# Projecting attention values and state-space gates with tokens on the partitions

## The chip, the cores and the metric

One NeuronCore of a Trainium2 chip runs the whole program. TensorE (PE) multiplies, VectorE (DVE) and ScalarE (ACT) work on its results in PSUM and on SBUF, GpSimd (POOL) helps, and SyncE (SP) issues most transfers. The metric is the device time of one execution in microseconds, the median of several.

## The reference

Two layers of a decoder trunk in float32, 512 tokens of 1024 features, batch 1. A layer, with W_in one projection whose columns are q, k, v, z, x, B, C, dt and two gates:

```python
x = x + 0.5 * swiglu(rms_norm(x, ffn1_norm[l]), ffn1_w_up[l], ffn1_w_down[l])
h = rms_norm(x, mix_norm[l])
q, k, v, z, xbc, dt_raw, gate_sb, gate_ssm = jnp.split(h @ w_in[l], IN_SPLITS, axis=-1)
y_sb = stick_breaking_attention(q, k, v) @ w_branch_sb[l]          # 4 heads of 128
y_ssm = mamba2_mixer(z, xbc, dt_raw, ...) @ w_branch_ssm[l]        # 24 heads of 64, 8 groups
x = x + (sigmoid(gate_sb) * y_sb + sigmoid(gate_ssm) * y_ssm) @ w_out[l]
x = x + 0.5 * swiglu(rms_norm(x, ffn2_norm[l]), ffn2_w_up[l], ffn2_w_down[l])
```

The mixer convolves x, B and C over four tokens per channel and applies silu, scans each group of three heads in chunks of 128 tokens, multiplies the result by silu(z), and normalises each group's 192 channels.

## The kernel before

**Layout.** Activations lie with features on the partitions: h is 8 tiles of 128 features by 512 tokens. A projection block (`project`) is 8 steps over the features; each step has three matmuls of 512 columns (`mm3`): every operand is split in a high part (hhi, whi) and a rest (hlo, wlo), and three of the four products are summed. The weights are the stationary operand (128x128), h the moving one, and the result, 128 features by 512 tokens, fills one PSUM tile "mm". The pool of these tiles has four, taken in turn: a block's tile is that of the block four earlier, and its first matmul waits until everything that reads the old one is done.

**Weights.** They come in units of up to 512 KB on SP's queue in the order of `unit_order`; ScalarE casts a unit to whi and VectorE subtracts (wlo, lines 259 and 261). Units are converted some blocks ahead.

**Order.** One thread of Python writes TensorE's stream block after block. What follows a block (scaling, convolution, attention, the scan) is a generator, given to `spawn`. After each step of a block `tick` advances all of them; so the order on every engine is set by how many ticks each generator lets pass (`yield n`). Engines run their own instructions in that order.

**The mixer.** q, k and v of four heads are projected in `qkv_order`. The first four blocks (q0, k0, q1, k1) are projected before the norm of x is known and scaled afterwards from PSUM by VectorE (lines 521 and 523, `scaled`). A v block is copied to SBUF by ScalarE and turned by `transposed` (line 834: four transposes on TensorE, which must go through PSUM), since attention needs tokens on the partitions; two splits (lines 380, 385) follow. Then come the 8 groups, 5 blocks each in GROUP_ORDER (3, 4, 0, 1, 2): B, C, x (128 columns), x and z (64 each), z (128), with two gate blocks between in the first six groups. `conv_block` does the convolution from PSUM: ScalarE the first tap (line 969), VectorE the others (line 972), then tanh on ScalarE (979) and the product that makes it silu on VectorE (989). Blocks 0 to 2 are transposed into "xz", x and z of the group by tokens; B also, in three quarters. `ssd_group` runs the scan of a group on all engines, in the end the norm (lines 1109 and 466 to 470, small operations, then 1119 on the normalised output), which is transposed back.

**The opening.** The first two blocks are computed while x and their weights arrive in pieces (`opening_loads`, `opening`, line 431).

Of the kernel before, what the change touches and what calls it, by code (L numbers as in the profile page):

```python
# [1 line left out]

# [56 lines left out]
NCONV = GROUPS * 4 * (KCONV + 1)  # L59


def group_cols(g):

    x0, z0 = OFF_X + g * GW, OFF_Z + g * GW
    b0, c0 = OFF_B + g * P, OFF_C + g * P
    return (list(range(x0, x0 + GW)) + list(range(z0, z0 + GW))
            + list(range(b0, b0 + P)) + list(range(c0, c0 + P)))
# [26 lines left out]
def unit_order(layer):  # L94
# [16 lines left out]
    for g in range(GROUPS):  # L111
        for i, c in enumerate(GROUP_ORDER):
            yield (layer, "grp", g, c), KB
            if g < EARLY and i in GATE_AT:
                yield (layer, GATE_AT[i], g), KB
    for m in range(EARLY, KB):
        yield (layer, "gs", m), KB
        yield (layer, "gm", m), KB
# [22 lines left out]
class Builder:  # L141
# [251 lines left out]
    def opening_loads(self):  # L393


# [3 lines left out]
        def weights(queue, i, cs):  # L399
            off, _ = self.units[self.keys[i]]  # L400
            src = self.wflat[off:off + KB * P * P].rearrange("(p f) -> p f", p=P)
            queue.dma_start(self.raw[i][:, cs], src[:, cs])
# [366 lines left out]
    def dt_stage(self, layer, ps):  # L769
# [54 lines left out]
        self.tok = self.t(mp, [P, NT, P], "tok", bufs=1)  # L824
# [12 lines left out]
    def qkv_parts(self, t, ps, normed, parts):  # L837
        scale = P ** -0.5 if t == "q" else None
        if normed and t != "v":
# [5 lines left out]
        if normed:  # L845
            self.nc.scalar.copy(r, ps)
        else:
            yield from self.scaled(r, ps, scale)
        yield 4 if t == "v" else 2
        if t == "v":  # L850
            r = self.transposed(r)
            yield 2
            two = self.pair(self.yt, ("yt", "yt"), (P, NT, P))
        else:
            two = self.pair(self.yt, ("yt", "yt"))
        yield from self.split(two, r)
        self.give("raw")
        parts[t] = two

# [5 lines left out]
    def attention(self, h, parts):  # L865
# [7 lines left out]
        at = [sum(SEQ - i * P for i in range(j)) for j in range(NT + 1)]  # L873
        spt = [self.t(mp, [P, at[NT]], "xz", F32R) for _ in range(2)]
        pzs, sps, ws, bufs, ready = {}, {}, {}, {}, set()

        def scores(j):
# [18 lines left out]
            yield from self.split([s[:, at[j]:at[j] + n] for s in spt], e)  # L896
            yield 2 if n < 300 else 3
            sps[j] = [s[:, at[j]:at[j] + n] for s in spt]
# [39 lines left out]
        while len(ws) < NT or "v" not in parts:  # L938
            yield 1
        yield 2  # L940
        v = parts["v"]
        po = self.t(self.ptr, [P, SEQ], "pt")
        for j in range(NT):
            self.mm3(po[:, j * P:], (v[0][:, j, :], v[1][:, j, :]), ws[j], j == 0, j == NT - 1,
# [6 lines left out]
    def conv_block(self, g, c, ps, proj):  # L951
# [5 lines left out]
        early = len(self.y_sb) < SBH or not self.dt_done  # L957
        src, scale = u, 1.0
        if c == 2:
            if early:  # L960
                nc.vector.tensor_copy(u, ps)
            else:
                src = ps
            scale = 0.5
            yield 1
        else:
            k0 = (g * 4 + (0, 1, None, 2, 3)[c]) * (KCONV + 1)
            tap = [self.conv[:, k0 + i:k0 + i + 1] for i in range(KCONV + 1)]
            nc.scalar.activation(u, ps, AF.Identity, scale=tap[KCONV - 1], bias=tap[KCONV])  # L969
            yield 2  # L970
            for i in range(1, KCONV):
# [456 lines left out]
```

## Time and profile before

| | |
|---|---|
| median of 3 runs | 2615.7 us (2614.91 to 2615.94) |
| the profiled execution | 2614.76 us |
| its span, first to last instruction | 2612.8 us |
| TensorE busy | 2593.7 us, 99% of the span |
| VectorE, ScalarE, GpSimd busy | 1752.5, 1298.2, 508.8 us |
| mean granted TensorE clock | 0.998 |

The busy time of an engine is the union of its instructions' times; a stretch in which TensorE is not busy is a wait. The profiled execution took 2.0 us more than its span. The mixer of layer 0 stands at about 356 to 860 us, that of layer 1 at about 1655 to 2155 us.

### The profile page before, as it was taken

To read this page: it belongs to the slowest core of one execution; us is meant where nothing else is said; L and a number is where in the kernel's file an instruction comes from. 1 tells how busy PE (TensorE), PEld (TensorE's weight loads), DVE (VectorE), ACT (ScalarE), POOL (GpSimd) and SP (SyncE) were. 2 spreads that over 40 slices of the span, in tenths; PEclk is the share of its full clock that TensorE was granted. 3 is DMA by queue.
4 is the path that set the end of the run, shared out by engine and by line. 5 is a ranking of instruction groups with operands and counts; after the bars stand their busy time and mean duration, and the time that the engine had idled before them with its cause. 6 is when DMAs were issued, how large, how long until landed. Compare 5 with 4: busy or idle time off the path is not lost.

```text
span 2612.8 us, 38174 instructions
## 1 busy us (share of the span) xinstructions
PE 2593.7 (99%) x15058; PEld 2294.1 (88%) x15058; DVE 1752.5 (67%) x2370; ACT 1298.2 (50%) x2095; POOL 508.8 (19%) x629
## 2 busy tenths in 40 slices
PE   9999999999999999999999999999999999999998
PEld 7898988888888889899998989888888888899997
DVE  7576876565665478585885858766666754775766
ACT  6343556655554255353553535566555643553434
POOL 1120201133232003021120312012332410021210
PEclk9999999999999999999999999999999999999999
DMA  5464442333323546463554644423333234464642
GB/s 186 138 155 138 122 137 77 102 109 105 113 89 100 163 145 162 137 182 110 160 141 126 176 126 130 134 77 107 97 117 105 97 101 157 137 179 131 175 122 81
DMA packets 104004, 336.37 MB, mean 129 GB/s; under 512 B 12128, under 2 KB 15456, under 8 KB 103824
## 3 DMA queue, kind: packets, MB, share of 16 engines
q1 hardware_dynamic: 91728, 293.22, 34.9%
q0 software_dynamic: 10944, 39.85, 8.6%
q8 instruction: 118, 1.93, 0.3%
q10 hardware_dynamic: 1152, 0.86, 0.1%
q14 instruction: 62, 0.51, 0.1%
HBM read 321.20 MB, written 12.68 MB: 128 GB/s over the span
## 4 chain that ended last, share of the span: by engine, by line
PE 93%; DVE 4%; ACT 1%; DMA 1%; issue 1%; POOL 0%; SPq 0%; DVEq 0%; ACTq 0%
PE mm L292 26%; PE mm L294 26%; PE mm L293 26%; PE pa L293 3%; PE pa L294 3%; PE pa L292 3%; PE pa L1071 1%; PE pt L834 1%; PE pa L908 1%; DVE wlo L261 1%; PE pa L1073 1%; PE pt L1056 1%; PE pt L1054 1%; DVE cv L972 0%; DMA x<-in_xT_dram 0%
## 5 line engine op out<-in xcount | busy, mean ns | idle before, releaser
L259 ACT CAST whi<-wraw 128x1024 fp32r<-128x1024 f32 (+2 forms) x434 | 434.2, 1001 | 592.9 <-PE mm L294 505.3
L292 PE MATMUL mm<-hhi,whi 128*128 128x512 f32 (+1 forms) x1856 | 679.6, 366 | 1.1 <-ACT hhi L480 1.1
L294 PE MATMUL mm<-hlo,whi 128*128 128x512 f32 (+1 forms) x1856 | 660.3, 356 | 0.1
L293 PE MATMUL mm<-hhi,wlo 128*128 128x512 f32 (+1 forms) x1856 | 658.6, 355 | 0.5 <-DVE wlo L261 0.5
L261 DVE TENSOR_TENSOR wlo<-wraw,whi 128x1024 fp32r<-128x1024 f32 (+2 forms) x434 | 542.3, 1250 | 168.2 <-ACT whi L259 167.5
L294 PEld LDWEIGHTS mm<-hlo,whi 128*128 128x128 f32 x1856 | 350.9, 189 | 52.0 <-DVE hlo L482 0.5
L293 PEld LDWEIGHTS mm<-hhi,wlo 128*128 128x128 f32 x1856 | 351.7, 189 | 44.4 <-issue 1.0
L292 PEld LDWEIGHTS mm<-hhi,whi 128*128 128x128 f32 x1856 | 351.5, 189 | 44.0 <-ACT hhi L480 1.5
L597 POOL TENSOR_TENSOR g<-g,rs 128x512 f32<-128x512 f32 x76 | 133.2, 1752 | 735.8 <-DVE g L604 715.1
L261 DVE TENSOR_TENSOR wlo<-s,whi 128x1024 fp32r<-128x1024 f32 x152 | 235.5, 1564 | 58.4 <-ACT whi L259 58.4
L292 PE MATMUL mm<-act,whi 128*128 128x512 f32 (+1 forms) x710 | 274.0, 386 | 0.0
L293 PE MATMUL mm<-act,wlo 128*128 128x512 f32 (+1 forms) x710 | 273.8, 386 | 0.0
L294 PE MATMUL mm<-act,whi 128*128 128x512 f32 (+1 forms) x710 | 273.6, 385 | 0.0
L292 PE MATMUL mm<-th,whi 128*128 128x256 f32 x912 | 258.1, 283 | 0.0
L293 PE MATMUL mm<-th,wlo 128*128 128x256 f32 x912 | 258.1, 283 | 0.0
L294 PE MATMUL mm<-tl,whi 128*128 128x256 f32 x912 | 258.1, 283 | 0.0
L259 ACT CAST whi<-s 128x1024 fp32r<-128x1024 f32 x152 | 159.0, 1046 | 100.4 <-PE mm L294 58.9
L623 DVE SCALAR_TENSOR_TENSOR x<-mm,x 128x512 f32<-128x512 f32 x93 | 64.0, 689 | 196.2 <-PE mm L294 196.2
L292 PEld LDWEIGHTS mm<-th,whi 128*128 128x128 f32 x912 | 175.1, 192 | 0.0
L293 PEld LDWEIGHTS mm<-th,wlo 128*128 128x128 f32 x912 | 175.1, 192 | 0.0
L294 PEld LDWEIGHTS mm<-tl,whi 128*128 128x128 f32 x912 | 175.1, 192 | 0.0
L972 DVE SCALAR_TENSOR_TENSOR cv<-mm,conv,cv 128x511 f32<-128x511 f32 (+2 forms) x192 | 142.3, 742 | 24.7 <-ACT cv L969 22.9
(275 smaller groups left out, 4566.6 us busy)
## 6 DMA issues: line engine op xcount, KB each, us to landing
wraw<-in_wflat_dram SPq DMA_DIRECT2D x354, 512.0 KB, 3.7
s<-in_wflat_dram SPq DMA_DIRECT2D x76, 512.0 KB, 5.4
s<-in_wflat_dram POOLq DMA_DIRECT2D x76, 512.0 KB, 9.1
wraw<-in_wflat_dram SPq DMA_DIRECT2D x64, 384.0 KB, 3.1
cumb<-cum_d SPq DMA_DIRECT2D x16, 768.0 KB, 3.9
xd<-x SPq DMA_DIRECT2D x16, 256.0 KB, 3.2
wraw<-in_wflat_dram SPq DMA_DIRECT2D x16, 256.0 KB, 3.1
x<-xd SPq DMA_DIRECT2D x16, 256.0 KB, 5.2
```

The source lines that it names most:

```text
L259: nc.scalar.copy(hi[:, :n], raw[:, :n])
L261: nc.vector.tensor_tensor(lo[:, :n], raw[:, :n], hi[:, :n].bitcast(F32), op=ALU.subtract)
L292: mm(ps, a[0], b[0], start=start, stop=False, **kw)
L293: mm(ps, a[1], b[0], start=False, stop=False, **kw)
L294: mm(ps, a[0], b[1], start=False, stop=stop, **kw)
L597: eng.tensor_tensor(r, r, self.rs[:, cols].unsqueeze(1).to_broadcast([P, 2, half]), op=ALU.mult)
L623: self.nc.vector.scalar_tensor_tensor(x, pd, 0.5, x, op0=ALU.mult, op1=ALU.add)
L834: self.nc.tensor.transpose(pt[:, cs], src[:, cs], self.ident)
L908: nc.tensor.matmul(pz[:, (i - j) * P:n], lhs, part, start=False, stop=(i == j and part is sps[i][1]), skip_group_check=True)
L972: nc.vector.scalar_tensor_tensor(u[:, i:], ps[:, :SEQ - i], tap[KCONV - 1 - i], u[:, i:], op0=ALU.mult, op1=ALU.add)
L1054: nc.tensor.matmul(pc[:, :P], bt[:, span(c)], ct[:, span(c)], start=True, stop=True)
L1056: nc.tensor.matmul(pu, btok[:, c, :], xws[c].rearrange("p h d -> p (h d)"), start=True, stop=True)
```

## The change

For v and z the operands of the matmul change places. `by_tokens` takes h as the stationary operand, 128 tokens at a time, and the weights as the moving one: 512 columns for v (all four heads), 384 for z (two groups, a pair). The result has 128 tokens on the partitions; four PSUM tiles, one for each 128 tokens, are opened in the first unit (256 features) and closed in the fourth and last. v is split straight from PSUM (`v_part`), z activated straight from it (`z_part`). The convolution blocks are whole 128-column blocks of x, three for a pair of groups, which are transposed and handed out to the two groups. The order of the blocks is written in `group_steps`: pair by pair, z within the pair, gate blocks where a 1 stands. All weights of z have units of 384 KB. In the opening all pieces of the two first weight units go on SP's queue; ScalarE's queue keeps the parameters. Some scratch tiles move to other pools.

```diff
-GROUP_ORDER = (3, 4, 0, 1, 2)
 EARLY = 6
-GATE_AT = {1: "gs", 3: "gm"}
...
+def group_steps():
+
+
+    gates = iter([(t, m) for m in range(EARLY) for t in ("gs", "gm")])
+    for p in range(GROUPS // 2):
+        a, b = 2 * p, 2 * p + 1
+        if p == 0:
+            steps = [("z", p), ("b", a), 1, ("c", a), ("x", 0), 1, ("x", 1), ("x", 2), 1, ("b", b), ("c", b), 1]
+        else:
+            steps = [("b", a), ("c", a), 1, ("x", 3 * p), ("x", 3 * p + 1), ("z", p), ("x", 3 * p + 2), p < 3,
+                     ("b", b), ("c", b), p < 2, p < 2]
+            if p == 3:
+                steps[2] = 0
+        for step in steps:
+            if step in (0, 1):
+                if step:
+                    yield next(gates)
+            else:
+                yield step
+    yield from gates
+    for m in range(EARLY, KB):
+        yield "gs", m
+        yield "gm", m
...
-    yield from (("q", 0), ("k", 0), ("q", 1), ("k", 1), ("v", 0), ("v", 1))
+
+    yield from (("q", 0), ("k", 0), ("q", 1), ("k", 1))
+    for u in range(NT):
+        yield "v", u
     for h in range(2, SBH):
-        yield from (("q", h), ("k", h), ("v", h))
+        yield from (("q", h), ("k", h))
...
-                weights(nc.sync if m else nc.scalar, i, slice(m * P, m * P + n))
+                weights(i, slice(m * P, m * P + n))
...
+    def by_tokens(self, done, n, *key):
+
+
+        assert self.normed
+        ps = []
+        for u in range(NT):
+            w = self.unit(*key, u)
+            for c in range(NT):
+                if u == 0:
+                    ps.append(self.t(self.pmm, [P, SEQ], "mm")[:, :n])
+                for k in range(2):
+                    ks, cs = slice(k * n, (k + 1) * n), slice(c * P, (c + 1) * P)
+                    self.mm3(ps[c], [t[:, cs] for t in self.h[2 * u + k]], [t[:, ks] for t in w],
+                             u + k == 0, u == NT - 1 and k == 1)
+                    if n == SEQ or c % 2 == 0 or k == 0:
+                        self.tick()
+                if u == NT - 1:
+                    self.spawn(done(c, ps[c]))
+
+    def v_part(self, c, ps):
+        two = self.pair(self.yt, ("yt", "yt"))
+        yield from self.split(two, ps)
+        self.v[c] = two
...
+    def z_part(self, p, c, ps):
+
+        nc = self.nc
+        while not self.room["z"]:
+            yield 1
+        self.room["z"] -= 1
+        z = self.t(self.mp, [P, 2 * GW], "z", bufs=NT)
+        if len(self.y_sb) < SBH or not self.dt_done:
+            nc.scalar.copy(z, ps)
+            yield from self.opened()
+            r = yield from self.take("raw")
+            nc.scalar.activation(r[:, :2 * GW], z, AF.Tanh, scale=0.5)
+            yield 1
+            nc.vector.scalar_tensor_tensor(z, r[:, :2 * GW], 1.0, z, op0=ALU.add, op1=ALU.mult)
+            self.give("raw")
+        else:
+            self.tables(False)
+            nc.scalar.activation(z, ps, AF.Tanh, scale=0.5)
+            yield 1
+            nc.vector.scalar_tensor_tensor(z, z, 1.0, ps, op0=ALU.add, op1=ALU.mult)
+        for g in (2 * p, 2 * p + 1):
+            self.ssm[g]["z", c] = z[:, g % 2 * GW:(g % 2 + 1) * GW]
...
-                    proj = {"done": set()}
-                    for i, c in enumerate(GROUP_ORDER):
-                        self.spawn(self.conv_block(g, c, self.project(layer, "grp", g, c)[0], proj))
-                        if g < EARLY and i in GATE_AT:
-                            open_gate(GATE_AT[i], g)
-                    self.spawn(self.ssd_group(layer, g, proj))
-                for m in range(EARLY, KB):
-                    gates[m] = [open_gate(t, m) for t in ("gs", "gm")]
+                    self.spawn(self.ssd_group(layer, g))
+                for kind, i in group_steps():
+                    if kind == "z":
+                        self.by_tokens(partial(self.z_part, i), 2 * GW, layer, "z", i)
+                    elif kind in ("gs", "gm"):
+                        gates.setdefault(i, []).append(open_gate(kind, i))
+                    else:
+                        self.spawn(self.conv_block(kind, i, self.project(layer, kind, i)[0]))
```

What it does on TensorE is seen best in its row of instructions. First the place in the mixer of layer 0 where k of head 1 (mm_3553) ends; before, v of head 0 (mm_3631) follows as one tile. Behind the arrow stand the moving operand and then the stationary one:

```order
L294 MATMUL mm_3553<-hlo_3446,whi_3478 128x512
L292 MATMUL mm_3631<-hhi_3559,whi_3522 128x512 [waits Activation_49]
L293 MATMUL mm_3631<-hhi_3559,wlo_3523 128x512 [waits DVE_49]
L294 MATMUL mm_3631<-hlo_3560,whi_3522 128x512 [waits DVE_49]
L292 MATMUL mm_3631<-hhi_3569,whi_3522 128x512 [waits Activation_49]
L293 MATMUL mm_3631<-hhi_3569,wlo_3523 128x512
L294 MATMUL mm_3631<-hlo_3570,whi_3522 128x512 [waits DVE_49]
```

All 24 matmuls of v of head 0 go into this tile. After, TensorE's row at the second to fourth tile of v (mm_3649, mm_3671, mm_3681), within the first unit, whi moving and hhi stationary:

```order
L318 MATMUL mm_3649<-whi_3522,hhi_3569 128x512
L319 MATMUL mm_3649<-whi_3522,hlo_3570 128x512
L320 MATMUL mm_3649<-wlo_3523,hhi_3569 128x512
L318 MATMUL mm_3671<-whi_3522,hhi_3559 128x512 [waits DVE_49]
L319 MATMUL mm_3671<-whi_3522,hlo_3560 128x512
L320 MATMUL mm_3671<-wlo_3523,hhi_3559 128x512
L318 MATMUL mm_3671<-whi_3522,hhi_3569 128x512
L319 MATMUL mm_3671<-whi_3522,hlo_3570 128x512
L320 MATMUL mm_3671<-wlo_3523,hhi_3569 128x512
L318 MATMUL mm_3681<-whi_3522,hhi_3559 128x512 [waits DVE_49]
L319 MATMUL mm_3681<-whi_3522,hlo_3560 128x512
L320 MATMUL mm_3681<-wlo_3523,hhi_3559 128x512
```

What moved: the third and the fourth tile are opened 12 and 18 matmuls after v's first, and each waits on VectorE. The operations that they wait for are the scaling of q of head 1 (from mm_3515) and of k of head 1 (from mm_3553), which stand in VectorE's row of the changed kernel like this; the row of before has the same operations in the same order:

```order
L358 TENSOR_TENSOR hlo_3613<-x_93,hhi_3612 128x512 [waits PE_49,Activation_49]
L548 SCALAR_TENSOR_TENSOR raw_3637<-pa_3432,rs_3496 128x512
L546 TENSOR_TENSOR raw_3639<-pa_3472,rs_3496 128x512
L548 SCALAR_TENSOR_TENSOR raw_3641<-mm_3515,rs_3496 128x512
L287 TENSOR_TENSOR wlo_3644<-wraw_3516,whi_3643 128x1024 [waits DMAHW3_49,Activation_49]
L411 TENSOR_TENSOR yt_3654<-raw_3637,yt_3653 128x512 [waits Activation_49]
L411 TENSOR_TENSOR yt_3657<-raw_3639,yt_3656 128x512 [waits Activation_49]
L411 TENSOR_TENSOR yt_3660<-raw_3641,yt_3659 128x512 [waits Activation_49]
L546 TENSOR_TENSOR raw_3669<-mm_3553,rs_3496 128x512 [waits DVE_49]
L411 TENSOR_TENSOR yt_3679<-raw_3669,yt_3678 128x512 [waits Activation_49]
```

Second, the z of a pair. Before, z blocks are transposed within the next block; here the set of one z block of layer 0 (cv_5619) in the middle of a later block's matmuls:

```order
L292 MATMUL mm_5612<-hhi_3591,whi_5527 128x512
L293 MATMUL mm_5612<-hhi_3591,wlo_5528 128x512
L294 MATMUL mm_5612<-hlo_3592,whi_5527 128x512
L834 MATMUL pt_5651<-ident,cv_5619 128x128 [waits DVE_49,PE_49]
L834 MATMUL pt_5651<-ident,cv_5619 128x128 x3
L1054 MATMUL pt_5656<-cT_5330,bT_5329 128x128 [waits Activation_49]
L1056 MATMUL pt_5656<-xw_5630,btok_5331 128x192 [waits Pool_49]
L292 MATMUL mm_5612<-hhi_3598,whi_5527 128x512
L293 MATMUL mm_5612<-hhi_3598,wlo_5528 128x512
L294 MATMUL mm_5612<-hlo_3599,whi_5527 128x512
```

There the transposes and a scan's step sit between two steps of one block. After, where z of pair 1 opens behind an x block (mm_5441): its first tile has six matmuls, and behind them stand the transposes of the x block before that one (cv_5451):

```order
L319 MATMUL mm_5441<-hhi_3612,wlo_5318 128x512
L320 MATMUL mm_5441<-hlo_3613,whi_5317 128x512
L318 MATMUL mm_5508<-whi_5401,hhi_3559 128x384 [waits Activation_49]
L319 MATMUL mm_5508<-whi_5401,hlo_3560 128x384
L320 MATMUL mm_5508<-wlo_5402,hhi_3559 128x384 [waits DVE_49]
L318 MATMUL mm_5508<-whi_5401,hhi_3569 128x384
L319 MATMUL mm_5508<-whi_5401,hlo_3570 128x384
L320 MATMUL mm_5508<-wlo_5402,hhi_3569 128x384
L859 MATMUL pt_5521<-ident,cv_5451 128x128 [waits DVE_49]
L859 MATMUL pt_5521<-ident,cv_5451 128x128 x3
L318 MATMUL mm_5526<-whi_5401,hhi_3559 128x384 [waits Activation_49]
L319 MATMUL mm_5526<-whi_5401,hlo_3560 128x384
```

The fourth tile of this z opens some rows further down, behind another set of transposes and the second and third tile, and waits for VectorE's last tap over mm_5441. VectorE's row there, from the end of a group's norm on (raw_5499 is the normalised output):

```order
L494 TENSOR_TENSOR gnt_5481<-gnt_5481,gny_5480 128x4 [waits DVE_49]
L495 SCALAR_TENSOR_TENSOR gny_5480<-gnt_5481,gny_5480 128x4 [waits DVE_49]
L1193 TENSOR_TENSOR raw_5499<-y_5200,gny_5480 128x512 [waits DVE_49,Pool_49]
L1024 SCALAR_TENSOR_TENSOR cv_5451<-raw_5450,cv_5451 128x512 [waits Activation_49]
L1012 SCALAR_TENSOR_TENSOR cv_5513<-mm_5441,conv_4218,cv_5513 128x511 [waits Activation_49]
L287 TENSOR_TENSOR wlo_5516<-wraw_5385,whi_5515 128x768 [waits DMAHW1_49,PE_49,Activation_49]
L1012 SCALAR_TENSOR_TENSOR cv_5513<-mm_5441,conv_4218,cv_5513 128x510 [waits DVE_49]
L1210 SCALAR_TENSOR_TENSOR yt_5547<-pt_5530,par_106,yt_5546 128x512 [waits Activation_49]
L1012 SCALAR_TENSOR_TENSOR cv_5513<-mm_5441,conv_4218,cv_5513 128x509 [waits DVE_49]
L1024 SCALAR_TENSOR_TENSOR cv_5513<-raw_5512,cv_5513 128x512 [waits Activation_49]
```

What moved: the taps of the x block just before z stand behind the norm and behind the activation of the x block ahead of it, and z's fourth tile waits for the last of them.

## Rows read from the trace of the kernel before

**Rows 1.** The page's head: the span, the busy time of each engine (share of the span, instructions) and, from the chain that ended last, its shares by engine.

```profile
span 2612.8 us, 38174 instructions
...
PE 2593.7 (99%) x15058; PEld 2294.1 (88%) x15058; DVE 1752.5 (67%) x2370; ACT 1298.2 (50%) x2095; POOL 508.8 (19%) x629
...
PE 93%; DVE 4%; ACT 1%; DMA 1%; issue 1%; POOL 0%; SPq 0%; DVEq 0%; ACTq 0%
```

**Rows 2.** What TensorE waited for, over the whole span: the line that waited and its releaser, then us in total, number of times, longest.

```profile
PE pt L1054 <- DVE yt L1136: 2.0, 2, 1.0
PE pt L834 <- DVE raw L1119: 1.3, 2, 0.7
PE pt L834 <- DVE cv L989: 1.2, 2, 0.6
...
PE pa L431 <- ACT hhi L480: 1.1, 1, 1.1
```

**Rows 3.** The timeline of TensorE's matmuls at one set of transposes between the matmuls of a projection (start us, us, engine, line, operation, out<-in, array and output, count).

```profile
537.38 0.39 PE L294 MATMUL mm<-hlo,whi 128*128 128x512 f32 x1
537.62 0.60 PE L834 MATMUL pt<-ident,cv 128*128 128x128 f32 x4
537.97 0.48 PE L292 MATMUL mm<-hhi,whi 128*128 128x512 f32 x1
538.29 0.39 PE L293 MATMUL mm<-hhi,wlo 128*128 128x512 f32 x1
```

**Rows 4.** The timeline of TensorE's matmuls at two triples of matmuls with 384 columns, in the attention of layer 0.

```profile
471.86 0.33 PE L292 MATMUL pt<-cT,yt 128*128 128x384 f32 x1
472.03 0.34 PE L293 MATMUL pt<-cT,yt 128*128 128x384 f32 x1
472.20 0.34 PE L294 MATMUL pt<-cT,yt 128*128 128x384 f32 x1
...
498.24 0.33 PE L292 MATMUL pt<-cT,yt 128*128 128x384 f32 x1
498.41 0.34 PE L293 MATMUL pt<-cT,yt 128*128 128x384 f32 x1
498.59 0.34 PE L294 MATMUL pt<-cT,yt 128*128 128x384 f32 x1
```

**Rows 5.** The timeline of TensorE's matmuls where k of head 1 ends and v of head 0 begins, layer 0.

```profile
378.67 0.39 PE L294 MATMUL mm<-hlo,whi 128*128 128x512 f32 x1
378.90 0.39 PE L292 MATMUL mm<-hhi,whi 128*128 128x512 f32 x1
```

**Rows 6.** The timeline of VectorE at the same time, layer 0. The first raw<-mm scales q of head 1, the second k of head 1.

```profile
378.57 3.09 DVE L332 TENSOR_TENSOR hlo<-x,hhi 128x512 fp32r<-128x512 f32 x5
...
382.79 0.68 DVE L523 SCALAR_TENSOR_TENSOR raw<-mm,rs 128x512 f32<-128x512 f32 x1
383.38 1.21 DVE L261 TENSOR_TENSOR wlo<-wraw,whi 128x1024 fp32r<-128x1024 f32 x1
384.51 1.89 DVE L385 TENSOR_TENSOR yt<-raw,yt 128x512 fp32r<-128x512 f32 x3
386.32 0.68 DVE L521 TENSOR_TENSOR raw<-mm,rs 128x512 f32<-128x512 f32 x1
```

**Rows 7.** The timeline of VectorE at the same place of layer 1: the same two scalings.

```profile
1677.14 0.68 DVE L523 SCALAR_TENSOR_TENSOR raw<-mm,rs 128x512 f32<-128x512 f32 x1
...
1680.68 0.68 DVE L521 TENSOR_TENSOR raw<-mm,rs 128x512 f32<-128x512 f32 x1
```

**Rows 8.** The timeline of all engines around the end of one projection block of a state-space group in layer 0: the normalisation of a group's output (from its first small operation to the normalised tile), the block's last matmul, ScalarE's first convolution pass over its PSUM tile (line 969), and VectorE's other taps over it (line 972), with a weight split between them.

```profile
571.52 0.17 DVE L1109 TENSOR_SCALAR ss<-ss 128x4 f32<-128x4 f32 x1 [1.89 <-ACT t L1089]
...
571.93 0.39 PE L294 MATMUL mm<-hlo,whi 128*128 128x512 f32 x1
...
572.36 0.78 ACT L969 ACTIVATE cv<-mm,conv 128x512 f32<-128x512 f32 x1 [0.87 <-PE mm L294]
...
573.76 0.69 DVE L1119 TENSOR_TENSOR raw<-y,gny 128x512 f32<-128x512 f32 x1
...
574.37 0.74 DVE L972 SCALAR_TENSOR_TENSOR cv<-mm,conv,cv 128x511 f32<-128x511 f32 x1
...
575.03 1.21 DVE L261 TENSOR_TENSOR wlo<-wraw,whi 128x1024 fp32r<-128x1024 f32 x1
...
576.17 1.52 DVE L972 SCALAR_TENSOR_TENSOR cv<-mm,conv,cv 128x510 f32<-128x510 f32 x2
```

**Rows 9.** The timeline of TensorE's matmuls at one wait in the mixer of layer 0.

```profile
546.04 0.60 PE L834 MATMUL pt<-ident,cv 128*128 128x128 f32 x4
547.65 0.49 PE L1054 MATMUL pt<-cT,bT 128*128 128x128 f32 x2 [1.01 <-DVE yt L1136]
```

**Rows 10.** The timeline of the opening: the weight loads on ScalarE's queue and the first matmuls.

```profile
1.27 0.93 ACTq L402 DMA_DIRECT2D wraw<-in_wflat_dram  x2
...
6.01 1.72 PE L431 MATMUL pa<-hhi,whi 128*128 128x512 f32 x2 [1.10 <-ACT hhi L480]
```

**Rows 11.** The chain that ended last, in order of time, in the opening (start us, us, what).

```profile
14.58 5.55 DMA wraw<-in_wflat_dram
20.23 1.05 ACT whi L259
```

**Rows 12.** VectorE's groups of instructions, shapes apart: line, operation, count | busy, mean ns | idle before, releaser.

```profile
L261 DVE TENSOR_TENSOR wlo<-wraw,whi 128x768 fp32r<-128x768 f32 x64 | 65.2, 1019 | 40.0 <-ACT whi L259 40.0
```

More of the change, by code (lines that the diff above doesn't have):

```diff
@@ L1 @@
 from contextlib import ExitStack
+from functools import partial
 import concourse.bass as bass
@@ L838, in qkv_parts @@
         scale = P ** -0.5 if t == "q" else None
-        if normed and t != "v":
+        if normed:
             two = self.pair(self.yt, ("yt", "yt"))
@@ L844, in qkv_parts @@
         r = yield from self.take("raw")
[L845 to L855, printed above, removed]
+        yield from self.scaled(r, ps, scale)
+        yield 2
+        two = self.pair(self.yt, ("yt", "yt"))
         yield from self.split(two, r)
@@ L858, in qkv_parts @@
         parts[t] = two
+    def by_tokens(self, done, n, *key):
+        assert self.normed
+        ps = []
+        for u in range(NT):
+            w = self.unit(*key, u)
[11 more added lines that the diff above has]
+    def v_part(self, c, ps):
+        two = self.pair(self.yt, ("yt", "yt"))
+        yield from self.split(two, ps)
+        self.v[c] = two
     def causal(self, ap, op):
@@ L872, in attention @@
         q, k = parts["q"], parts["k"]
-        at = [sum(SEQ - i * P for i in range(j)) for j in range(NT + 1)]
-        spt = [self.t(mp, [P, at[NT]], "xz", F32R) for _ in range(2)]
+        rest = self.t(mp, [P, 2, SEQ - P], "xs", F32R, bufs=3)
+        short = self.t(mp, [P, 2, P], "short", F32R, bufs=1)
+        spt = []
+        for i in range(2):
+            long = self.t(mp, [P, SEQ + 2 * P], "xs", F32R, bufs=3)
+            spt.append([long[:, :SEQ], rest[:, i, :], long[:, SEQ:], short[:, i, :]])
         pzs, sps, ws, bufs, ready = {}, {}, {}, {}, set()
@@ L895, in scores @@
             yield 1
-            yield from self.split([s[:, at[j]:at[j] + n] for s in spt], e)
+            yield from self.split([s[j] for s in spt], e)
             yield 2 if n < 300 else 3
-            sps[j] = [s[:, at[j]:at[j] + n] for s in spt]
+            sps[j] = [s[j] for s in spt]
         def weights(j):
@@ L949, in attention, with opened, conv_block @@
         self.y_sb.append(two)
-    def conv_block(self, g, c, ps, proj):
+    def opened(self):
+        while len(self.y_sb) < SBH or not self.dt_done:
+            yield 1
+        self.tables(False)
+    def conv_block(self, kind, i, ps):
         nc, mp = self.nc, self.mp
@@ L956, in conv_block @@
         u = yield from self.take("cv")
[L957 to L964, printed above, removed]
-            yield 1
[L966 to L971, printed above, removed]
-                nc.vector.scalar_tensor_tensor(u[:, i:], ps[:, :SEQ - i], tap[KCONV - 1 - i], u[:, i:],
-                                               op0=ALU.mult, op1=ALU.add)
-                yield 1
-            yield 1
-        while len(self.y_sb) < SBH or not self.dt_done:
-            yield 1
-        self.tables(False)
-        nc.scalar.activation(r, src, AF.Tanh, scale=scale)
+        _, k0 = conv_at(kind, i)
+        tap = [self.conv[:, k0 + j:k0 + j + 1] for j in range(TAPS)]
+        nc.scalar.activation(u, ps, AF.Identity, scale=tap[KCONV - 1], bias=tap[KCONV])
+        yield 2
+        for j in range(1, KCONV):
+            nc.vector.scalar_tensor_tensor(u[:, j:], ps[:, :SEQ - j], tap[KCONV - 1 - j], u[:, j:],
+                                           op0=ALU.mult, op1=ALU.add)
+            yield 1
+        yield 1
+        yield from self.opened()
+        nc.scalar.activation(r, u, AF.Tanh)
         yield 1
@@ L1010, in ssd_group @@
         h0 = g * HPG
-        while self.ssd_on or not {0, 1, 3, 4} <= proj["done"]:
+        proj = self.ssm[g]
+        while self.ssd_on or not {"c", "btok", ("x", g % 2), ("x", 1 + g % 2)} <= set(proj):
             yield 1
@@ L1339, in lay_out @@
         dt_w[:, :, :HEADS] = w_in[:, None, OFF_DT:OFF_DT + HEADS]
-        grp = [w_in[:, group_cols(g)] for g in range(GROUPS)]
         for key, n in unit_order(layer):
```

126 lines of the change are left out of this document (72 added, 54 removed).

## The prediction

> **What bounds the kernel now.** I read the page's busy shares first, then the chain that ended last, then TensorE's waits, then the timelines of the places that the change touches. The page gives TensorE 2593.7 of 2612.8 us and 93% of the chain [rows 1]: it is the bound, and almost nothing else is. Its waits come to single microseconds [rows 2]. So a change here is worth what it takes out of TensorE's own stream, less what TensorE then waits for. The unit of that stream is the distance from one start to the next. A matmul of 512 columns takes 0.227 us (378.67 to 378.90) [rows 5]; one of 384 columns 0.170 in one set of three (471.86 to 472.20, two steps) and 0.175 in another (498.24 to 498.59), 0.173 on the mean [rows 4]; the duration printed beside a matmul is longer, since they overlap.
>
> **What a set of transposes costs.** Four 128x128 transposes between projection matmuls: the matmul ahead starts at 537.38, the second one behind the set at 538.29 [rows 3]. That is 0.91 us, where two steps of 0.227 would be 0.45. A set adds 0.46 us: the four themselves, and a first matmul behind them that is held to 0.32.
>
> **Removed.** With tokens on the partitions, v needs no transposes (4 sets in a layer) and z none (it was one and a half of the three 128-column blocks of a group, but x and z together now need one set for each of 12 x blocks in place of 24: 12 sets fewer). 16 sets in a layer, 32 in all: 32 x 0.46 = **-14.6 us**.
>
> **Added matmuls.** v keeps its number and its 512 columns. z was 12 blocks of 24 matmuls with 512 columns in a layer, and is 16 units of 24 with 384. 768 x 0.173 = 132.9 against 576 x 0.227 = 130.8: **+2.1 us**, between -0.2 (0.170) and +3.6 (0.175, the two ends of [rows 4]). A 384-column matmul is not three quarters of one with 512: each pays something that doesn't scale. [...]
>
> **What v then waits for.** This is the largest new term. Before, v was four projections with one PSUM tile each, and the tile of a projection came free while others were computed. Now four PSUM tiles are opened within one unit: six matmuls into each, all four held until the last unit. The pool has four tiles in a ring, so the third is that of q1 and the fourth that of k1, both still waiting for VectorE's scaling. In the trace k1's last matmul starts at 378.67 and v's first at 378.90 [rows 5]; the third tile is wanted 12 x 0.227 = 2.72 us later, at 381.62. VectorE is then in an unbroken run of work [rows 6]: five hlo of the normed input, the scalings, q1's at 382.79 for 0.68, so q1's tile is free at 383.47. Wait: 1.85. Six matmuls on, at 384.83, the fourth is wanted; k1's scaling stands behind a weight split and three yt, starts at 386.32 and ends at 387.00. Wait: 2.17. VectorE's order at this place is the same as before, so its times should be. Together 4.0 us; layer 1 has the same two scalings at the same distance [rows 7]: **+8.0 us**, between 6 and 9. Everything behind it on TensorE moves with it, and nothing can go ahead. What is late next is only VectorE's work on v itself, which has 18 matmuls, some 4 us, before q2 wants the first of these tiles.
>
> **What z waits for.** A z step again takes the ring's four tiles within 18 x 0.173 = 3.1 us of its first matmul, and the fourth is that of the x block just ahead. A convolution block holds its tile long: in one case the last matmul starts at 571.93, ScalarE's first pass at 572.36, and VectorE's third tap ends at 576.17 + 1.52 = 577.69 [rows 8], 5.76 us later, with small operations and a normalisation ahead of the first tap (571.52 to 574.45) and a weight split of 1.2 us between the taps. With z's narrower split, 1.0 us [rows 12], and without the normalisation in the way (1.2 us), it would be 4.3 to 4.6. TensorE wants the tile 0.23 + 3.1 us after that last matmul and later by 0.46 for each set of transposes that falls in between.
> Pair 0 opens while attention still runs, and its x blocks come later; no wait. Pair 1: the normalisation run stands ahead of the activation of the x block before last, whose transposes are in TensorE's row after z's first six matmuls. I place it 2.4 us after z's start, from 2.9 us for the run and the taps ahead of it, against 1.04: a wait of 1.3. The taps of the last x block come behind it: 0.7 + 0.9 + 0.7 + 0.7 + 0.8 more is about 6.3, where TensorE is at 1.0 + 1.3 + 0.46 + 1.04 + 0.46 + 1.04 = 5.3 with the fourth tile: 1.0 to 1.3. Pair 1 costs 2.5 in a layer. Pairs 2 and 3: one insertion and no run in the way, 4.4 less 3.8: 0.65 each. Near the end, the transposes of group 6's normalised output stand where the b block of group 7 has its taps in the same run: 0.9. Both layers: 2 x (2.5 + 0.65 + 0.7 + 0.9) = **+9.5 us**. None of these waits is in the trace before; below they reach to nothing if VectorE's queue is empty enough, above to the 5.76 us of [rows 8] everywhere.
>
> **Waits of before that go.** Three places in each layer [rows 2]: 2.0 + 1.3 + 1.2 = 4.5 us of counted wait. The step shows more than the count: a set at 546.04 should be followed after 0.36, at 546.40, and is at 547.65 [rows 9], 1.25 where 1.01 is counted. With 0.2 for each of six, **-5.8 us**; nothing, if the same operations wait at their new places.
>
> **The opening.** Two weight loads go from ScalarE's queue to SP's, first and third there, so the first x comes second. The first matmul at 6.01 waits for hhi of that x [rows 10]. It might start up to a microsecond earlier or later, but TensorE isn't the end here: the chain runs over x's loads, a weight load from 14.58 of 5.55 us, ScalarE's split at 20.23 [rows 11] and onward on VectorE. The bytes ahead of that load are the same. **0**, between -1 and +1. [...]
>
> **The sum.** -14.6 + 2.1 + 8.0 + 9.5 - 5.8 + 0 = -0.8 us against the profiled execution's 2614.8 (span 2612.8 and 2.0 around it): 2614.0. The median of the runs shown, 2615.7, is 0.9 above that one. A measurement of this kernel can tell 0.2%, 5.2 us, from no change: faster is under 2610.5, slower over 2620.9.
>
> **The rivals.**
> *z hardly waits.* If TensorE's wait at v gives VectorE the time to be ahead from there on, and the taps run as fast as [rows 8] allow without anything between (0.43 + 0.78 + 3 x 0.75 = 3.5 us), the 9.5 falls to about 1: 2605.5, faster. For it: VectorE is busy 67% of the time only [rows 1]. Against: its work comes in bursts, and the run of rsqrt steps is one. Chance 0.25.
> *v does not wait either.* 2614.0 - 9.5 - 8.0 = 2596.5. Against it stands the unbroken run of [rows 6]. Chance 0.06.
> *z's fourth tile is the new bound (slower).* If the normalisation run and a weight split fall between the taps at pairs 1 to 3, as in [rows 8], the tile is free after 5.8 and up to 8 us where it is wanted after 3.3 to 4.3: 1.5 to 4 us at each of six places, 9 to 24 in place of the 7.7 counted there. 6.9 us more than counted make it slower than before; at 3.5 each it is 2627. For it: that is what the rows show for one block. Against: of pair 1's run most is over when z starts. Chance 0.17.
> *The waits of before come back* at their new places: 2614.0 + 5.8 = 2619.8, no measurable change. Chance 0.12.
> *The forecast itself*, terms within a few microseconds: 0.40, its own range 2609 to 2620.
>
> **How the numbers follow.** Faster: the first two rivals and a fifth of the forecast's cases, 0.39. Slower: the third and little else, 0.19. The rest, 0.42, is no change. The range leaves out the second rival and the upper half of the third: 2599 to 2625.
>
> **What would show it.** In the profile after: 128 transposes fewer, 768 matmuls with 384 columns 0.173 apart; TensorE waits at v's third and fourth tile for VectorE's scaling of q1 and k1, about 1.9 and 2.2 us, in both layers; at z's fourth tile for the third tap of an x block, longest in pair 1, with pair 0 free of it; the waits for yt, raw and cv of [rows 2] smaller. The prediction is wrong if VectorE's scalings come earlier than in [rows 6], if the step of a 384-column matmul differs here, or if TensorE's waits at z are of another size than 0.6 to 2.5 us.

## The result and the profile after

The changed kernel takes 2627.06 us (2626.31 to 2627.47), the kernel before 2615.36 beside it: ratio 1.0045, interval 1.003 to 1.0059. It is slower by 11.7 us; 2614.0 was forecast, with a range up to 2625.

The page's head of the changed kernel, which answers to [rows 1]:

```profile
span 2625.5 us, 38311 instructions
...
PE 2588.9 (99%) x15122; PEld 2307.6 (88%) x15122; DVE 1748.9 (67%) x2362; ACT 1280.8 (49%) x2087; POOL 506.9 (19%) x629
...
PE 90%; DVE 6%; ACT 2%; issue 1%; DMA 1%; POOL 0%; SPq 0%; DVEq 0%; ACTq 0%
```

TensorE is busy 4.8 us less than before, as was meant, but the span is 12.7 longer: 36.6 us without a matmul in place of 19.1. TensorE's waits in the changed kernel (line, releaser, us in total, times, longest), to be held against [rows 2]:

```profile
PE mm L318 <- DVE cv L1012: 4.8, 6, 1.0
PE mm L318 <- DVE raw L546: 3.8, 2, 1.9
PE mm L318 <- DVE raw L548: 3.5, 2, 1.7
PE pt L859 <- DVE raw L1193: 2.5, 2, 1.2
PE pt L859 <- DVE bT L1024: 2.4, 4, 0.6
PE pt L859 <- DVE cv L1024: 2.2, 4, 1.0
...
PE pa L1142 <- DVE dec L1133: 1.3, 2, 0.7
```

The lines are those of the changed file: 318 to 320 are `mm3`, 859 the transposes, 1012 a convolution tap, 1024 the product that ends a convolution block's activation, 1193 a group's normalised output, 1133 a step of the scan (dec), 546 and 548 the scaling of k and q. The first three rows are PSUM tiles of z and v, the next three transposes.

**v.** TensorE's matmuls from the second to the fourth tile of v in layer 0:

```profile
381.79 0.39 PE L320 MATMUL mm<-wlo,hhi 128*128 128x512 f32 x1
383.92 0.50 PE L318 MATMUL mm<-whi,hhi 128*128 128x512 f32 x1 [1.75 <-DVE raw L548]
...
385.19 0.39 PE L320 MATMUL mm<-wlo,hhi 128*128 128x512 f32 x1
387.46 0.70 PE L318 MATMUL mm<-whi,hhi 128*128 128x512 f32 x1 [1.89 <-DVE raw L546]
387.96 0.63 PE L319 MATMUL mm<-whi,hlo 128*128 128x512 f32 x1
388.39 0.63 PE L320 MATMUL mm<-wlo,hhi 128*128 128x512 f32 x1
...
390.95 0.43 PE L320 MATMUL mm<-wlo,hhi 128*128 128x512 f32 x1
391.21 0.39 PE L318 MATMUL mm<-whi,hhi 128*128 128x512 f32 x1
```

The third tile starts 2.13 us behind the matmul ahead of it, the fourth 2.27: less a step of 0.227, 1.91 and 2.05 are lost, where 1.85 and 2.17 were forecast. But look at the starts behind 387.46: after one step of 0.50, seven are 0.43 long (387.96 to 388.39, and so on to 390.95); from 391.21 on they are 0.23 again. The windows of the same stretch (us, then busy time of PE, PEld, DVE, ACT, POOL; PE's granted clock; DMA share, GB/s):

```profile
385.00:387.00 2.00, 0.58 (x3) 0.15 (x1) 2.00 (x5) 0.00 (x0) 0.00 (x0) 1.00 0.49 80
387.00:389.00 2.00, 1.54 (x4) 1.25 (x5) 1.10 (x2) 0.62 (x1) 0.00 (x0) 0.65 0.46 182
389.00:391.00 2.00, 2.00 (x7) 1.52 (x6) 0.00 (x0) 1.04 (x1) 0.00 (x0) 0.50 0.00 0
391.00:393.00 2.00, 2.00 (x12) 1.71 (x11) 1.23 (x1) 0.59 (x2) 0.00 (x0) 1.00 0.00 0
```

The granted clock is 1.00 until 387, then 0.65 on the mean of two us, then 0.50, and 1.00 again from 391. TensorE had stood still for 1.75 and 1.89 us with six matmuls between. Layer 1 shows the same at 1688 to 1691 (0.52 on the mean from 1688 to 1690). The slow steps cost 1.7 us in layer 0 and 1.5 in layer 1, counted from one start to the next. No wait is shown for them: TensorE counts as busy, 2.00 of 2.00 us from 389 to 391.

**z.** TensorE at z of pair 1, layer 0:

```profile
581.68 0.34 PE L319 MATMUL mm<-whi,hlo 128*128 128x384 f32 x1
581.86 0.34 PE L320 MATMUL mm<-wlo,hhi 128*128 128x384 f32 x1
583.16 0.66 PE L859 MATMUL pt<-ident,cv 128*128 128x128 f32 x4 [0.97 <-DVE cv L1024]
...
586.02 0.34 PE L320 MATMUL mm<-wlo,hhi 128*128 128x384 f32 x1
587.31 0.41 PE L318 MATMUL mm<-whi,hhi 128*128 128x384 f32 x1 [0.95 <-DVE cv L1012]
```

and VectorE ahead of the two late starts:

```profile
581.81 0.69 DVE L1193 TENSOR_TENSOR raw<-y,gny 128x512 f32<-128x512 f32 x1
582.42 0.69 DVE L1024 SCALAR_TENSOR_TENSOR cv<-raw,cv 128x512 f32<-128x512 f32 x1
583.51 0.75 DVE L1012 SCALAR_TENSOR_TENSOR cv<-mm,conv,cv 128x511 f32<-128x511 f32 x1 [0.40 <-ACT cv L1009]
...
586.42 0.74 DVE L1012 SCALAR_TENSOR_TENSOR cv<-mm,conv,cv 128x509 f32<-128x509 f32 x1
```

The transposes of cv come 1.13 late (the activation's product ends at 583.11, behind the normalised output that line 1193 writes), z's fourth tile 1.12 late (the third tap ends at 587.16). Together 2.25 us, where 2.5 were forecast. The 384-column step is 0.18 here (581.68 to 581.86); the mean of 600 undisturbed ones in the trace is 0.174.

**The b blocks**, which the prediction passed over. TensorE, then VectorE, between z of pair 1 and z of pair 2:

```profile
631.52 0.39 PE L320 MATMUL mm<-hlo,whi 128*128 128x512 f32 x1
632.51 0.55 PE L859 MATMUL pt<-ident,bT 128*128 128x128 f32 x3 [0.60 <-DVE bT L1024]
```

```profile
627.02 0.75 DVE L1210 SCALAR_TENSOR_TENSOR yt<-pt,par,yt 128x512 fp32r<-128x512 f32 x1 [2.61 <-ACT yt L1208]
...
629.48 1.53 DVE L1012 SCALAR_TENSOR_TENSOR cv<-mm,conv,cv 128x510 f32<-128x510 f32 x2
631.76 0.69 DVE L1024 SCALAR_TENSOR_TENSOR bT<-raw,cv 128x512 f32<-128x512 f32 x1 [0.76 <-ACT raw L1017]
```

The three transposes of bT follow a matmul at 631.52 and could start at 631.75; VectorE's activation of bT begins at 631.76 only, since it waits for ScalarE's tanh, which waits for the third tap (629.48 + 1.53). TensorE loses 0.76 us. VectorE isn't short of time here: it stood idle for 2.61 us until 627.02. The operation at 627.02 makes the rest (lo) of a group's normalised output (line 1210) and waits for ScalarE, which makes the high part (line 1208); the b block's first tap stands behind it in VectorE's row. The same operation, after 3.97 and 2.62 us of idle time, stands ahead of the taps of the other two b blocks that TensorE waits for.

**Where it went, layer 0's mixer.** From the sum over the last norm's rows ahead of the mixer to that behind it, both included, the span grew from 604.99 to 610.78 us, by 5.8; layer 1's grew by 5.85. Every distance from one start to the next on TensorE, sorted (us; counts in brackets, before and after):

| | before | after | difference |
|---|---|---|---|
| transposes (188, 124) | 17.3 | 11.4 | -5.9 |
| first matmul held behind an insertion (97, 86) | 7.8 | 6.8 | -1.0 |
| 512 columns (2256, 1968) at 0.227, 384 columns (24, 408) at 0.173 | 516.3 | 517.3 | +1.1 |
| stops and slow steps over 0.12 us | 3.6 | 14.7 | +11.1 |
| all else | 60.0 | 60.6 | +0.6 |

Matmuls of 512 and 384 columns are counted at a fixed 0.227 and 0.173; what their steps differ from that is under "all else". The 14.7 are: v's tiles 3.96, the slow clock 1.67, z and cv in pair 1 2.25, z's fourth tile in pairs 2 and 3 0.68 and 1.09, the normalised output of group 6 1.39, three b blocks 1.79, one scan step waiting for dec 0.77, the first x block's transposes 0.33, and 0.73 that before has too.

### The profile page after: what moved, and what is told of

The parts are those of the page before. It is cut to its first block, busy times and chain, and to the rows that moved or that the text cites. A ratio compares the mean times of both kernels' runs of the same rounds, so it can differ in the third digit from the quotient of the medians.

```text
span 2625.5 us, 38311 instructions
## 1 busy us (share of the span) xinstructions
PE 2588.9 (99%) x15122; PEld 2307.6 (88%) x15122; DVE 1748.9 (67%) x2362; ACT 1280.8 (49%) x2087; POOL 506.9 (19%) x629
## 3 DMA queue, kind: packets, MB, share of 16 engines
q8 instruction: 119, 1.95, 0.3%
## 4 chain that ended last, share of the span: by engine, by line
PE 90%; DVE 6%; ACT 2%; issue 1%; DMA 1%; POOL 0%; SPq 0%; DVEq 0%; ACTq 0%
PE mm L318 25%; PE mm L320 25%; PE mm L319 25%; PE pa L320 3%; PE pa L319 3%; PE pa L318 3%; DVE wlo L287 2%; PE pa L1142 1%; DVE cv L1012 1%; ACT whi L285 1%; PE pa L953 1%; PE pt L859 1%; PE pa L1144 1%; PE pt L1127 1%; PE pt L1125 0%
## 5 line engine op out<-in xcount | busy, mean ns | idle before, releaser
L318 PE MATMUL mm<-hhi,whi 128*128 128x512 f32 (+1 forms) x1600 | 575.0, 359 | 1.1 <-ACT hhi L505 1.1
L319 PE MATMUL mm<-hhi,wlo 128*128 128x512 f32 (+1 forms) x1600 | 559.9, 350 | 2.1 <-DVE wlo L287 2.1
L320 PE MATMUL mm<-hlo,whi 128*128 128x512 f32 (+1 forms) x1600 | 560.8, 351 | 0.1
L320 PEld LDWEIGHTS mm<-hlo,whi 128*128 128x128 f32 x1600 | 303.1, 189 | 40.9 <-DVE hlo L507 0.5
L319 PEld LDWEIGHTS mm<-hhi,wlo 128*128 128x128 f32 x1600 | 303.7, 190 | 39.1 <-DVE wlo L287 3.3
L318 PEld LDWEIGHTS mm<-hhi,whi 128*128 128x128 f32 x1600 | 303.6, 190 | 38.0 <-DVE z L1069 1.6
L320 PEld LDWEIGHTS mm<-act,whi 128*128 128x128 f32 x710 | 133.5, 188 | 26.7
```

The costliest lines, as they stand in the source:

```text
L318: mm(ps, a[0], b[0], start=start, stop=False, **kw)
L319: mm(ps, a[1], b[0], start=False, stop=False, **kw)
L320: mm(ps, a[0], b[1], start=False, stop=stop, **kw)
```

## The experiments

The kernel before, run again beside them, has medians of 2614.9 to 2615.2 us. Where a mixer's length is given, it goes from the start of one of those sums over a norm's rows to the start of the next: 604.5 us in layer 0 and 604.4 in layer 1 before, 610.3 in both after.

**Opening undone.**

```diff
-                weights(i, slice(m * P, m * P + n))
+                weights(nc.sync if m else nc.scalar, i, slice(m * P, m * P + n))
```

> The changed kernel with the opening alone undone: the first two weight pieces go on ScalarE's queue again. In the trace of the changed kernel the first projection matmul starts at 5.12 us where it was 6.01 before, and the matmul that waits longest in the opening ends its wait at 53.9 where it was 53.5. Theory: the opening is worth 0.4 us or less of loss, so this gives 2626.5 to 2627.1 (changed kernel: 2627.1). Rival: the earlier start is worth its 0.9 us and something else took it, then this is slower, about 2628.

2626.92 us (2626.28 to 2628.28), no difference to 2627.06. The opening is worth nothing that can be measured. In the trace of the changed kernel the first projection matmul starts 0.9 us earlier (5.12 for 6.01), and the wait for a weight split at its end takes that back and a little more:

```profile
53.90 0.51 PE L319 MATMUL mm<-hhi,wlo 128*128 128x512 f32 x1 [1.56 <-DVE wlo L287]
54.23 0.40 PE L320 MATMUL mm<-hlo,whi 128*128 128x512 f32 x1
54.48 0.40 PE L318 MATMUL mm<-hhi,whi 128*128 128x512 f32 x1
```

The matmul at 53.90 stood at 53.53 in the trace before. A difference of 0.4 here says little: in the nine traces with the changed opening the mixer of layer 0 begins anywhere between 362.5 and 364.0 us.

**v later.**

```diff
-    yield from (("q", 0), ("k", 0), ("q", 1), ("k", 1))
-    for u in range(NT):
-        yield "v", u
     for h in range(2, SBH):
         yield from (("q", h), ("k", h))
+        if h == 2:
+            for u in range(NT):
+                yield "v", u
```

> The changed kernel with v's four units after q and k of head 2 instead of after k of head 1; nothing else is changed. Its four PSUM tiles are then those of q1, k1, q2 and k2, of which the first two are long scaled. Theory: both waits at v (2.0 and 2.0 us in a layer against the step of 0.227) and the stretch behind them with a granted clock of 0.5 (1.7 us in a layer) go: 2 x 5.6 = 11.3 us, 2615.8. Rival A: VectorE is what is short there, and the wait only moves to the tiles of q2 and k2: over 2621. Rival B: the low clock comes from the swapped operands and not from the waits: then 1.7 us in a layer stay, 2619.2, with a granted clock of 0.5 in v.

2616.06 us (2615.05 to 2616.98); 2615.8 was expected. TensorE's row has no wait at v, its granted clock is 1.00 from 381 to 397 us and 0.998 on the mean of the span, as before (0.997 in the changed kernel), and the waits at z are what they were:

```profile
PE mm L319 <- DVE cv L1013: 4.8, 6, 1.0
PE pt L860 <- DVE raw L1194: 2.5, 2, 1.2
PE pt L860 <- DVE bT L1025: 2.4, 4, 0.6
```

4.8, 2.5 and 2.4 us, to the tenth the figures of the changed kernel. Its mixers take 604.7 us each. So v's wait was a matter of its place, it did not move elsewhere, and the swapped operands alone didn't lower the clock.

**The waits filled.**

```diff
+                    if n == SEQ and c > 1:
+                        warm = self.t(self.ptr, [P, SEQ], "pt")
+                        for _ in range(8):
+                            self.nc.tensor.matmul(warm[:, :P], self.ones, self.ones, start=True, stop=True)
                     ps.append(self.t(self.pmm, [P, SEQ], "mm")[:, :n])
```

> The changed kernel with eight small matmuls (128x128, a result that nobody reads) ahead of the third and ahead of the fourth PSUM tile of v, 1.7 us of work each, inside the waits of 1.75 and 1.89 us. The waits for VectorE stay what they are, the third tile starts at the same time. Theory: TensorE's clock falls because it stood still twice in a short time; with the waits filled it stays, and the nine slow matmuls of each layer run at 0.227 again: 1.7 us in a layer, 2627.1 - 3.4 = 2623.7, granted clock 1.00 in the stretch. Rival: the clock falls for another reason (the swapped operands, a stretch of VectorE work), and it is 2627 to 2628 with the same slow stretch.

2624.37 us (2623.81 to 2625.0), 2.7 under the changed kernel; 3.4 was expected. The projection matmuls around the filled waits, and the windows behind them:

```profile
382.32 0.40 PE L320 MATMUL mm<-wlo,hhi 128*128 128x512 f32 x1
...
384.45 0.50 PE L318 MATMUL mm<-whi,hhi 128*128 128x512 f32 x1
...
385.71 0.39 PE L320 MATMUL mm<-wlo,hhi 128*128 128x512 f32 x1
...
387.99 0.50 PE L318 MATMUL mm<-whi,hhi 128*128 128x512 f32 x1
```

```profile
384.00:387.00 3.00, 3.00 (x21) 2.59 (x20) 3.00 (x5) 1.05 (x2) 0.00 (x0) 1.00 0.25 35
387.00:389.00 2.00, 1.90 (x12) 1.56 (x12) 1.31 (x3) 0.62 (x1) 0.00 (x0) 1.00 0.54 209
389.00:391.00 2.00, 2.00 (x11) 1.61 (x10) 0.71 (x2) 1.05 (x1) 0.00 (x0) 1.00 0.00 0
```

The distances 382.32 to 384.45 and 385.71 to 387.99 are 2.13 and 2.28, as without the filling (2.13 and 2.27): VectorE sets them, whose two scalings end at 384.39 and 387.94. The small matmuls take 1.95 us in each of the two waits. The clock stays at 1.00. Same waits, no slow steps: the clock followed TensorE's standing still. Its price for both layers is 2.7 us by the medians, 3.0 by the mixers (1.5 shorter each) and 3.2 by the slow steps of the trace.

**v alone undone** (four blocks and their transposes as before, z by tokens).

```diff
-        if normed:
+        if normed and t != "v":
...
+        if t == "v":
+            r = self.transposed(r)
```

> The changed kernel with v alone undone: four v blocks with features on the partitions and a set of transposes each, as before; z, the pairs and the opening as changed. Theory: v's waits and the slow stretch (11.3 us in both layers) go, eight sets of transposes come back (8 x 0.456 = 3.6 us): 2619.4, and the rest over the kernel before, 4 us, is z's waits less its transposes. Rival: v's waits give VectorE room which z's part lives on, and z then waits more: 2622 or over.

2620.23 us (2619.03 to 2620.68), near the 2619.4 expected. What is left of the change (z, the order of the blocks, the opening) is thus 5.1 us slower than before. TensorE's waits at z are again 4.8, 2.5, 2.4 and 2.2 us, so they didn't depend on the time that v's waits gave VectorE. No run separates z's layout from the order of the blocks.

**A gate before z** (from here on with v later).

```diff
-            steps = [("b", a), ("c", a), 1, ("x", 3 * p), ("x", 3 * p + 1), ("z", p), ("x", 3 * p + 2), p < 3,
+            steps = [("b", a), ("c", a), p < 3, ("x", 3 * p), ("x", 3 * p + 1), 1, ("z", p), ("x", 3 * p + 2),
...
-            if p == 3:
-                steps[2] = 0
```

> The kernel with v later (2616.1) with one more edit: in pairs 1 to 3 a gate block is put between the second x block and z, so that z's fourth PSUM tile is that of the gate, which ScalarE alone reads, and its third that of the x block. Theory: the waits at z's fourth tile for an x block's third tap (1.05 + 0.64 + 1.04 us in a layer) go: 2 x 2.7 = 5.5 us, 2610.6. Rival: a convolution block holds its tile so long that the third tile then waits in its place, or the gate missing elsewhere costs as much: 2614 to 2618, with waits of 0.6 to 1 us at z's third tile or at the blocks that lost their gate.

2613.52 us (2612.57 to 2615.37): 2.5 gained of 5.5. The wait at z's fourth tile is gone from the list, as the theory has it. The rival had the rest: not at z's third tile, but further behind z, where pairs 1 and 2 now lack a gate. The transposes of a normalised output wait in the c block there (1.2 us by the starts), and those of b in the block after it:

```profile
PE pt L858 <- DVE raw L1192: 6.3, 6, 1.1
PE pt L858 <- DVE bT L1023: 3.7, 6, 0.8
PE pt L858 <- DVE cv L1023: 1.6, 4, 0.7
```

TensorE waits for the normalised output three times in a layer now, 6.3 us in place of 2.5, and for b 3.7 in place of 2.4.

**Later transposes.**

```diff
-        yield 2
+        yield 4 if kind == "b" else 2
...
-            yield 3
+            yield 6 if src is yn else 3
```

> The kernel with v later (2616.1) with one more edit: the transposes of a b block are put two steps (1.4 us) further down TensorE's row and those of a group's normalised output three steps (2.0 us). Nothing else is changed. Theory: TensorE waits there only because these transposes stand too early in its row for VectorE: the waits for bT (0.28 + 0.77 + 0.77) and for the normalised output (1.41) go, 3.2 us in a layer, 6.4 in both: 2609.7. Rival: VectorE itself is late there, and what it is late with shows at the next tile or the next transposes: 2613 to 2616.

2608.14 us (2607.25 to 2609.34), 7.9 gained where 6.4 were expected. The rows for bT and the normalised output are gone, and that for dec with them (0.8 us in a layer), which the theory hadn't counted; left are:

```profile
PE mm L319 <- DVE cv L1013: 4.4, 6, 0.9
PE pt L860 <- DVE cv L1025: 2.7, 4, 1.0
```

That these transposes only stood too early for VectorE may be half of it. With the normalised output transposed later, its rest (line 1211 here) comes later too, and no longer holds up the taps of b:

```profile
621.64 0.74 DVE L1211 SCALAR_TENSOR_TENSOR yt<-pt,par,yt 128x512 fp32r<-128x512 f32 x1
```

It stands behind the block's last two taps (620.20 for 1.52) now, and the product for bT ends 6.3 us behind the block's last matmul in place of 8.2. The two edits of this run weren't tried one by one.

**Both.** 

> The kernel with v later and both edits: the gate before z, and the later transposes. Theory: the waits are separate and the gains add: 5.5 + 6.4 = 11.9 us under 2616.1, 2604.2, faster than the kernel before by 11. Rival: the gains share VectorE's backlog; 2608 or more.

2607.7 us (2607.31 to 2608.39), 8.4 gained in place of 11.9: the gains do not add, as the rival has it. With z's tile and those transposes out of the way, the x blocks' transposes wait instead, ten times:

```profile
PE pt L858 <- DVE cv L1023: 9.4, 10, 1.2
```

**x blocks later too**, once with the gate before z and once without.

```diff
-        yield 4 if kind == "b" else 2
+        yield 4
```

> The kernel with v later, the gate before z and the later transposes (2607.7), with the transposes of x blocks also two steps (1.4 us) later. What TensorE still waits for in its mixers is the activation of an x block ahead of its transposes: 0.57 + 0.83 + 1.39 + 1.37 + 1.37 us in a layer. Theory: these transposes too only stand too early, and the waits go: 5.5 us in a layer, 11 in both, 2596.7 to 2599. Rival: the backlog of VectorE moves on once more, to a PSUM tile of a projection, and takes half or more: 2603 to 2608.

2602.88 us (2602.01 to 2603.26), ratio to before 0.9954 (0.9939 to 0.9969): 12 us under before, 24 under the changed kernel. 4.8 of 11 expected; the rival's end of 2603 is nearer than the theory's. What is left in the mixers (597.9 and 597.7 us) is small:

```profile
PE pt L1124 <- DVE state L1134: 1.8, 2, 1.1
PE mm L317 <- DVE z L1068: 1.6, 6, 0.3
```

The x blocks' waits went as the theory says; the two rows are new. From one start to the next these stops take 2.5 us in layer 0 and 2.2 in layer 1, which is most of what the spans lack of the 11 (2605.9 to 2600.1, 5.8 less): the wait moved on once more, to the scan's state and to the tile that z's first token block leaves to the next projection.

> The kernel with v later and the later transposes (2608.1), the gates where the change has them, with the transposes of x blocks also two steps later. Theory: the waits for an x block's activation go (0.57 + 1.12 + 0.16 us in a layer), those at z's fourth tile stay (1.03 + 0.54 + 1.10) since a PSUM tile can't be read earlier: 2608.1 - 3.7 = 2604.4. Rival: the x transposes gave VectorE time to finish the taps, and z's fourth tile waits longer by what they no longer wait: 2606 to 2608.

2606.72 us (2606.38 to 2607.48), as the rival has it: the transposes no longer wait, and z's fourth tile waits longer, 6.3 us after 4.4. A wait for the scan's state, 1.4 us, is new here too.

```profile
PE mm L319 <- DVE cv L1013: 6.3, 6, 1.6
```

**The remedy without the change** (kernel before, convolution transposes two steps later, normalised output three).

> The kernel before with the transposes of every convolution block two steps later and those of the normalised output three: the remedy without the change. The kernel before waits at three places in a mixer, 2.8 us in a layer; one of them (1.2 us) is for a product on VectorE behind the transposes. Theory: the two waits ahead of transposes (0.7 + 0.8 us in a layer) go, 2615.2 - 3.0 = 2612, so that the layout with tokens on the partitions keeps an advantage of its own of some 5 us or more once its waits are gone. Rival: the later transposes gain as much here as there, and the layout is worth nothing: 2608 or less.

2611.52 us (2610.99 to 2612.77), 3.4 gained where 3.0 were expected. The two waits ahead of transposes are gone, as the theory has it; the third, which it left standing, is gone too, and one new wait has come:

```profile
PE mm L292 <- DVE cv L989: 1.0, 2, 0.5
```

With v and z by tokens and the steps placed for it, 2602.9 is 8.6 below that: the layout is worth its transposes, if little waits. The kernel before was given one such remedy and the changed one several, but there is little left to remove in the former: its mixers (602.4 and 602.3 us) stop only there, 0.7 us in a layer by the starts.

## Why the prediction was wrong

- **Transposes removed, 32 sets at 0.46.** Right: -6.9 us in a layer were measured (-5.9 and -1.0), -7.3 forecast; 16 sets are gone but only 11 held matmuls, since some sets stood next to other insertions, where one is paid anyway.
- **384 columns.** Right: +1.1 in a layer counted at 0.173 a step, 1.3 with the 0.174 of the trace's mean; +1.05 was forecast. Part of a step doesn't scale with its columns in this trace: 0.227 us for 512, 0.174 for 384 where three quarters would be 0.170, 0.120 for 256 where half would be 0.114.
- **v's waits.** Mechanism and size right: 3.96 in a layer, 4.0 forecast, from VectorE's unchanged order. The step that failed is the sentence on them that "everything behind it on TensorE moves with it": I priced that at the wait alone. Behind the two stops the granted clock went from 1.00 to 0.50, which cost 1.7 us more in one layer and 1.5 in the other; with the stops filled it stayed at 1.00. The prediction counts every step of v at 0.227 us.
- **z's waits, "+9.5".** The second step that failed. The listed places were right in kind: pair 1 2.25 (2.5), pair 2 0.68 (0.65), pair 3 1.09 (0.7), group 6 1.39 (0.9): 5.4 in a layer for 4.75. What failed is the list. I asked which transposes and tiles stand near z, and priced every other place at nothing: the transposes of b blocks wait three times (1.8); a scan step waits for dec (0.8), the first x block 0.3. That is 2.9 us in a layer, 5.8 in all. Behind the b waits stands VectorE's row, not its load: it is idle ahead of their taps. That the new order of the blocks brought them is argued, not shown.
- **Waits of before, "-5.8".** Its own numbers (4.5, and 0.2 for each of six) give 5.7, and at their old places they went, 2.7 in layer 0. But only the wait for yt went for good. For normalised outputs TensorE now waits 2.5 us in place of 1.3, for products ahead of transposes 2.2 in place of 1.2, which the sum has among z's waits. So the rival that these waits come back at new places was right in kind for two of the three.
- **The opening, 0.** Right, as far as the experiment can tell.
- **The rivals.** That z hardly waits, and that v doesn't, were wrong. The slower rival put z's fourth tile at up to 2627. That 2627 was measured is chance: the fourth tile cost 2.9 us in a layer in all, and the way there led over the clock and the b blocks instead.

In one sum: forecast -0.4 in a layer; 1.7 for the clock, 2.9 for unlisted waits, 0.7 for those sized too low, 0.35 for the transposes, 0.6 for small differences: +5.85, against 5.8 measured in layer 0. What remains of the 12.7 us between the two spans, 1.0, lies outside the mixers: 0.4 ahead of the first, 0.6 behind the second. Traces of kernels that are the same there differ by about as much.

## What to carry to other kernels

Opening several PSUM tiles at once asks for tiles that the blocks just ahead still hold (1.75 and 1.89 us of waiting at v): lay the ring out by hand, and put such a step behind blocks whose readers are long done or short. When TensorE is the bound, an operation on it that depends on another engine may be better placed late; a few steps of delay took 8 us out here. But waits that hang on the same rows of VectorE and ScalarE need not add, 8.4 us gained of 11.9 here: look after each removal for what waits next. An engine that comes late need not be busy, as VectorE was idle for 2.61 us ahead of the taps of a b block: see first whether it stood idle behind an operation that waits for a third engine.

## What the runs showed of the hardware

A stop of TensorE can cost twice. After 1.75 and 1.89 us of standing still, six matmuls between, its granted clock was 0.50 for the following matmuls (0.43 us a step in place of 0.227), in both layers and again, in layer 0, with the opening undone; with small matmuls of no use in the same waits it was 1.00. How long it is low isn't fixed: in the changed kernel's trace seven steps of 0.43 us in each layer; with the opening undone, in layer 0, the granted clock was already 0.74 on the mean from 384 to 387, and 0.50 from 387 to 391. Nor must the clock have fallen when TensorE resumes: in layer 1 of the changed kernel the fourth tile's first step took 0.35 us (1687.66 to 1688.01), as the third tile's first did with the clock at 1.00 (1684.12 to 1684.47), the next 0.36, and only then came seven of 0.43. One stop of 1.56 us in the opening, at 53.90, had no such effect: 0.25 us (54.23 to 54.48) and then 0.23 a step behind it, the clock at 1.00 until 60. Nor had the two at z of pair 1, 0.97 and 0.95 us with 20 matmuls and transposes between: the granted clock was 1.00 in the four us behind them.
